# Casting two more weight groups by quarter lanes in a batched matmul, so that two loops cover 26 and 28 groups

## The chip, the cores and the metric

The kernel runs on one core of one Trainium2 chip. The metric is the device time of one execution in microseconds (us). A profile's span is some 1.8 us shorter than the time of the same execution (516.8 and 518.58 us for the kernel before), so spans are compared with spans and times with times. One run of the kernel before, at 660.4 us with a span of 658.6, counts as slow and is left out.

## The reference

```python
b1, b2, m, k, n = 8, 16, 256, 512, 384
x      = randn(b1, b2, m, k)  float32
weight = randn(b1, b2, k, n)  float32
out    = matmul(x, weight)    float32
```

There are 128 matrix products. The kernel takes four of them as one group, so there are 32 groups (`NG`), numbered 0 to 31.

## The kernel before

Each group loads 2048 KB of x and 3072 KB of weights, casts both to bf16, transposes x on TensorE, multiplies, and stores 1536 KB. The weights have two buffers (`WS = 2`), so group n can only be loaded when group n - 2 has been cast. All loads and stores are issued in program order on one queue, by SyncE.

The weights are cast in one of two forms. In the *long* form (`cast_w`, called by quarter lanes in the prediction) 16 casts of 32 partitions are shared: 11 on VectorE (`CV`) and 5 on ScalarE (`CA`), and the load is one transfer. In the *short* form (`cast_short`, by half lanes) 8 casts of 64 partitions run on VectorE alone, and the load is two transfers, so that the first four casts can start when the first half has landed. Before the change, groups 0 to 3, 30 and 31 are short.

```python
    def is_short(n):
        return isinstance(n, int) and (n < LAG or n >= NG - 2)      # LAG = 4

    def load_w(e, t, U, s):
        n = t * U + s
        if not isinstance(n, int) or n >= WS:
            e.wait_ge(w_vcast, n * CV + (1 - WS) * CV)              # group n-2 cast
            e.wait_ge(w_acast, n * CA + (1 - WS) * CA)
        d = SL // SH if is_short(n) else 1                          # two transfers or one
        ...

    def on_sync(e):
        ...
            for s in range(U):
                load_x(e, t, U, LAG + s)
                store(e, t, U, s)
                load_w(e, t, U, LAG + s)
        ...
        for n in range(NG - 1 - LAG, NG):                           # stores of 27 to 31
            store(e, 0, NG, n, T if n == NG - 1 else 1)             # the last in four pieces

    def on_vector(e):
        ...
        def step(t, U, s):
            n = t * U + s
            if is_short(n):
                cast_short(e, n)
            else:
                cast_w(e, t, U, s, range(XV))                       # 8 of the 11 casts
            if not isinstance(n, int) or n < NG - 1:
                next_x(t, U, s)                                     # x of group n+1
            if not is_short(n):
                cast_w(e, t, U, s, range(XV, CV), False)            # the other 3
        ...
        for n in range(LAG):
            step(0, NG, n)
        rounds = (NG - 3 - LAG) // U                                # 24 groups in the loop
        with e.Fori(0, rounds) as t:
            for s in range(U):
                step(t, U, LAG + s)
```

The store of a group waits for ScalarE's four copies out of PSUM. The store of group 31 goes out in four pieces of 384 KB, one after each copy.

Of the kernel before, what the change touches and what calls it, by code (L numbers as in the profile page):

```python
# [12 lines left out]
def kernel(  # L13
# [32 lines left out]
    NG = B // G  # L46

    XS, WS, OS = 2, 2, 4
    BS, TS, WBS = 1, 2, 2 * G
    PT, PO = 4, 2  # L50

    LAG = 4

    CA = 5
    CV = G * SL - CA
# [16 lines left out]
    def sems(name, n):  # L72
        return [tc.alloc_semaphore(f"{name}{s}") for s in range(n)]
# [23 lines left out]
    x_in, w_in, o_out = sems("x_in", XS), sems("w_in", WS), sems("o_out", OS)  # L97
# [6 lines left out]
    def load_x(e, t, U, s):  # L104
        n = t * U + s
        if not isinstance(n, int) or n >= XS:
            e.wait_ge(x_cast, n * T + (1 - XS) * T)
        e.dma_start(  # L108
            x_sb[s % XS][:],
            x_rows[bass.ds(n * (G * M), G * M)].rearrange("(p r) k -> p r k", r=R),  # L110
        ).then_inc(x_in[s % XS], 16)

    def is_short(n):
        return isinstance(n, int) and (n < LAG or n >= NG - 2)

    def load_w(e, t, U, s):
        n = t * U + s
        if not isinstance(n, int) or n >= WS:
            e.wait_ge(w_vcast, n * CV + (1 - WS) * CV)
            e.wait_ge(w_acast, n * CA + (1 - WS) * CA)  # L120
        d = SL // SH if is_short(n) else 1
        k = SL * KO // d
        for h in range(d):
            sem = h_in[s % WS * 2 + h] if is_short(n) else w_in[s % WS]
            e.dma_start(  # L125
                w_sb[s % WS][:, h * k : (h + 1) * k, :],
                w_rows[bass.ds(n * (G * K) + h * (G // d * K), G // d * K)].rearrange(
                    "(p k) n -> p k n", k=k
                ),
            ).then_inc(sem, 16)  # L130

    def store(e, t, U, s, pieces=1):
        n = t * U + s
        dram = o_rows[bass.ds(n * (G * M), G * M)].rearrange("(p r) n -> p r n", r=R)
        for q in range(pieces):
            rows = slice(q * R // pieces, (q + 1) * R // pieces)
            e.wait_ge(o_copied, n * T + ((q + 1) * T // pieces + BIAS))
            e.dma_start(out=dram[:, rows], in_=out_sb[s % OS][:, rows]).then_inc(
                o_out[s % OS], 16
            )  # L140

    def cast_x(e, t, U, s, q):
        n = t * U + s
        if q == 0:
            e.wait_ge(x_in[s % XS], (t * (U // XS) + s // XS) * 16 + 16)
        e.wait_ge(t_made, n * T + (q + 1 - T + BIAS))  # L146
        rows = slice(2 * q, 2 * q + 2)
        S = SH if is_short(n) else SL
        e.tensor_copy(  # L149
            out=x_bf[s % BS][:, rows].rearrange("p r (s q c) -> p r s q c", s=S, c=KO),  # L150
            in_=x_sb[s % XS][:, rows].rearrange("p r (q s c) -> p r s q c", s=S, c=KO),
        ).then_inc(x_cast, 1)

    def cast_w(e, t, U, s, parts, first=True):
        n = t * U + s
        if first:
            e.wait_ge(p_made, n * T + (BIAS - T))
            e.wait_ge(w_in[s % WS], (t * (U // WS) + (s - LAG) // WS) * 16 + 16)  # L158
        copy = e.tensor_copy if e is nc.vector else e.copy
        for c in parts:  # L160
            i, h = c // SL, c % SL
            copy(  # L162
                out=w_bf[(s * G + i) % WBS][h * C : (h + 1) * C],
                in_=w_sb[s % WS][i * C : (i + 1) * C, h * KO : (h + 1) * KO, :],
            ).then_inc(w_vcast if c < CV else w_acast, 1)

    def cast_short(e, n):
        e.wait_ge(p_made, n * T + (BIAS - T))
        p = P // SH
        for d in range(SL // SH):  # L170
            turns = n // WS if n < LAG else LAG // WS
            e.wait_ge(h_in[n % WS * 2 + d], turns * 16 + 16)  # L172
            for a in range(SH):
                for h in range(SH):
                    c = d * 4 + a * 2 + h
                    r = (d * SH + h) * KO

                    e.tensor_copy(  # L178
                        out=w_bf[(n * G + d * SH + a) % WBS][h * p : (h + 1) * p],
                        in_=w_sb[n % WS][a * p : (a + 1) * p, r : r + KO, :],  # L180
                    ).then_inc(w_vcast, 2 if c < CV - HV else 1)

    def evacuate(e, t, U, s):
        n = t * U + s
        e.wait_ge(p_made, n * T + (BIAS - T))
        for q in range(T):
            e.wait_ge(t_made, n * T + (q + 1 + BIAS))
            e.copy(  # L188
                out=x_t[s % TS][:, 2 * q : 2 * q + 2],
                in_=pt[(s * T + q) % PT][:].bitcast(bf16),  # L190
            ).then_inc(t_copied, 1)
# [36 lines left out]
    def copy_out(e, t, U, s, q):  # L228
        n = t * U + s
        if q == 0:  # L230
            e.wait_ge(o_out[s % OS], (t * (U // OS) + s // OS) * 16 + 16)
        e.wait_ge(p_made, n * T + (q + 1 + BIAS))
        e.copy(  # L233
            out=out_sb[s % OS][:, 2 * q : 2 * q + 2, :],
            in_=po[(s * T + q) % PO][:, :, :N],
        ).then_inc(o_copied, 1)
# [7 lines left out]
    def on_sync(e):  # L244
        U = OS
        for n in range(LAG):
            load_x(e, 0, NG, n)
            load_w(e, 0, NG, n)
        rounds = (NG - 2 - LAG) // U
# [4 lines that stand above are left out]
# [12 lines left out]
    def on_vector(e):  # L266
        U = 2

        def next_x(t, U, s):
            for q in range(T):  # L270
                cast_x(e, t, U, s + 1, q)
# [6 lines that stand above are left out]
                cast_w(e, t, U, s, range(XV))  # L278
            if not isinstance(n, int) or n < NG - 1:
                next_x(t, U, s)  # L280
            if not is_short(n):
                cast_w(e, t, U, s, range(XV, CV), False)

        next_x(0, NG, -1)
        for n in range(LAG):
            step(0, NG, n)
        rounds = (NG - 3 - LAG) // U
        with e.Fori(0, rounds) as t:  # L288
            for s in range(U):
                step(t, U, LAG + s)  # L290
        for n in range(LAG + rounds * U, NG):
            step(0, NG, n)

    def on_tensor(e):
# [14 lines left out]
    def on_scalar(e):  # L309
        U = OS  # L310
        e.sem_inc(t_copied, BIAS)
        e.sem_inc(o_copied, BIAS)
        for s in range(OS):
            e.sem_inc(o_out[s], 16)



        def step(t, U, s):
            short = is_short(t * U + s + 1)
            evacuate(e, t, U, s + 1)  # L320
            for q in range(T):
                copy_out(e, t, U, s, q)
                if q == 0 and short:
                    e.sem_inc(w_acast, CA)
                if q > 0 and not short:
                    last = CA if q == T - 1 else q
                    cast_w(e, t, U, s + 1, range(CV + q - 1, CV + last), q == 1)

        evacuate(e, 0, NG, 0)
        e.sem_inc(w_acast, CA)  # L330
        for n in range(LAG - 1):
            step(0, NG, n)
        rounds = (NG - 2 - LAG) // U
        with e.Fori(0, rounds) as t:
            for s in range(LAG - 1, LAG - 1 + U):
                step(t, U, s)
        for n in range(LAG - 1 + rounds * U, NG - 1):
            step(0, NG, n)
        for q in range(T):
            copy_out(e, 0, NG, NG - 1, q)  # L340

    on_gpsimd(nc.gpsimd)
    on_sync(nc.sync)
    on_vector(nc.vector)
    on_tensor(nc.tensor)
    on_scalar(nc.scalar)


# [28 lines left out]
```

## Time and profile before

In lines of a profile PE is TensorE and PEld its weight loads, DVE is VectorE, ACT is ScalarE, and SPq is SyncE issuing a transfer; L125 is a line of the kernel's file.

| | before |
|---|---|
| time, median of 3 runs | 518.49 us (518.26 to 518.54) |
| span of the profiled run | 516.8 us |
| TensorE, VectorE, ScalarE busy | 61%, 77%, 79% |
| data queue, share of 16 DMA engines | 99.0% (218.11 MB) |
| weight casts on VectorE: long, short | 286 of 951 ns, 48 of 955 ns |
| weight casts on ScalarE | 130 of 1468 ns |
| last copy out of PSUM ends | 506.57 us |
| last DMA increment lands | 515.3 us |

No engine computes after 506.57, and yet data moves for almost 9 us more. The trace also holds, for every transfer, 16 increments of its semaphore (1680 for 105 transfers). I read them as one for each of the 16 DMA engines, since in the tail 15 of the last piece's 16 are in at 512.28, the last comes at 515.31, and the DMA share between the two is 0.06, one engine of 16. The spread between the first and the last of them then tells how far the slowest engine lags.

### The profile page before, as it was taken

How to read it: one execution, taken by the hardware profiler on the slowest of the kernel's cores; microseconds unless marked ns; L12 is line 12 of the kernel's file. 1: busy time of each engine (PE TensorE's matmuls, PEld its weight loads, DVE VectorE, ACT ScalarE, POOL GpSimd, SP SyncE). 2: the span in 40 equal slices, each digit the busy share in tenths (PEclk: the TensorE clock that was granted, in tenths of full speed). 3: DMA queues.
4: the chain of work that ended last, by engine and by line, in shares of the span. 5: the costliest groups of instructions: out<-in, count | busy, mean ns of one | idle time of the engine just before them, and what ended most of it. 6: DMA issues, size and time to landing. Idle time of an engine off the chain costs nothing.

```text
span 516.8 us, 11572 instructions
## 1 busy us (share of the span) xinstructions
PE 315.2 (61%) x4608; PEld 225.4 (44%) x4608; DVE 397.7 (77%) x462; ACT 410.3 (79%) x387; POOL 0.7 (0%) x6
## 2 busy tenths in 40 slices
PE   2277838555676675765475766558656667565681
PEld 2255525444454443454353544435534445344550
DVE  2788757798777897777987778977779777797960
ACT  1365666998797989798979879978989897899561
POOL 0000000000000000000000000000000000000000
PEclk9687786878786778787778868776867786688887
DMA  8999999999999999999999999999999999999995
GB/s 335 426 428 425 435 429 423 431 430 434 429 424 431 432 439 434 424 426 433 434 434 431 422 432 433 435 429 428 425 438 429 440 428 420 433 433 429 424 428 219
DMA packets 15127, 218.19 MB, mean 422 GB/s; under 512 B 1680, under 2 KB 1680, under 8 KB 2192
## 3 DMA queue, kind: packets, MB, share of 16 engines
q1 hardware_dynamic: 15120, 218.11, 99.0%
q8 instruction: 3, 0.05, 0.0%
q14 instruction: 4, 0.03, 0.0%
HBM read 167.77 MB, written 50.33 MB: 422 GB/s over the span
## 4 chain that ended last, share of the span: by engine, by line
DMA 57%; DVE 29%; issue 9%; PE 1%; SPq 1%; DVEq 1%; ACT 0%
DMA w_sb<-in_weight_dram 57%; DVE w_bf L162 20%; DVE x_bf L149 5%; DVE w_bf L178 4%; PE po L219 1%; SPq L125 0%; DVEq L288 0%; SPq L108 0%; DVEq L158 0%; ACT out_sb L233 0%; SPq L120 0%; DVEq L146 0%; DVEq L172 0%; SPq L372 0%; SPq L60 0%
## 5 line engine op out<-in xcount | busy, mean ns | idle before, releaser
L162 DVE CAST w_bf<-w_sb 32x1536 bf16<-32x1536 f32 x286 | 271.9, 951 | 81.6 <-DMA w_sb<-in_weight_dram 73.5
L219 PE MATMUL po<-w_bf,x_t 128*32 128x384 bf16 x4096 | 200.6, 359 | 38.3 <-DVE w_bf L162 21.0
L201 PE MATMUL pt<-identity,x_bf 128*128 128x128 f32 x512 | 115.0, 415 | 152.2 <-DVE x_bf L149 152.2
L162 ACT CAST w_bf<-w_sb 32x1536 bf16<-32x1536 f32 x130 | 190.9, 1468 | 6.0 <-DMA w_sb<-in_weight_dram 2.8
L201 PEld LDWEIGHTS pt<-identity,x_bf 128*128 128x128 f32 x512 | 103.4, 224 | 164.1 <-issue 163.8
L219 PEld LDWEIGHTS po<-w_bf,x_t 128*32 128x32 bf16 x4096 | 122.0, 106 | 115.9 <-issue 40.7
L233 ACT COPY out_sb<-po 128x768 f32<-128x768 f32 x128 | 101.5, 803 | 57.3 <-PE po L219 56.6
L188 ACT COPY x_t<-pt 128x1024 bf16<-128x1024 bf16 x128 | 120.3, 1025 | 22.1 <-PE pt L201 21.5
L149 DVE CAST x_bf<-x_sb 128x1024 bf16<-128x1024 f32 x128 | 80.0, 688 | 12.4 <-DMA x_sb<-in_x_dram 11.5
L178 DVE CAST w_bf<-w_sb 64x1536 bf16<-64x1536 f32 x48 | 45.9, 955 | 8.3 <-DMA w_sb<-in_weight_dram 7.0
L188 ACT ACT_TABLE_LOAD x1 | 1.3, 1283 | 10.8 <-PE pt L201 10.8
masks.py:199 POOL TENSOR_SCALAR_AFFINE_SELECT identity<-identity 128x128 f32<-128x128 f32 x1 | 0.3, 294 | 0.2 <-POOL identity L239 0.2
L239 POOL MEMSET identity<- 128x128 f32 x1 | 0.2, 205 | 0.5 <-SPq L60 0.5
L361 POOL MEMSET const-bfloat16-1.0<- 128x1 bf16 x1 | 0.1, 102 | 0.0
L361 POOL MEMSET const-uint8-127<- 128x1 uint8 x1 | 0.1, 102 | 0.0
L361 POOL MEMSET const-float32-0.0<- 128x1 f32 x1 | 0.1, 99 | 0.2 <-issue 0.2
L361 POOL MEMSET const-float32-1.0<- 128x1 f32 x1 | 0.1, 99 | 0.0
## 6 DMA issues: line engine op xcount, KB each, us to landing
w_sb<-in_weight_dram SPq DMA_DIRECT2D x26, 3072.0 KB, 18.1
x_sb<-in_x_dram SPq DMA_DIRECT2D x32, 2048.0 KB, 22.3
out_dram<-out_sb SPq DMA_DIRECT2D x31, 1536.0 KB, 25.4
w_sb<-in_weight_dram SPq DMA_DIRECT2D x12, 1536.0 KB, 16.6
out_dram<-out_sb SPq DMA_DIRECT2D x4, 384.0 KB, 5.6
```

Source lines behind the costliest of these rows:

```text
L149: e.tensor_copy(out=x_bf[s % BS][:, rows].rearrange("p r (s q c) -> p r s q c", s=S, c=KO), in_=x_sb[s % XS][:, rows].rearrange("p r (q s ...
L162: copy(out=w_bf[(s * G + i) % WBS][h * C : (h + 1) * C], in_=w_sb[s % WS][i * C : (i + 1) * C, h * KO : (h + 1) * KO, :],).then_inc(w_vcas ...
L178: e.tensor_copy(out=w_bf[(n * G + d * SH + a) % WBS][h * p : (h + 1) * p], in_=w_sb[n % WS][a * p : (a + 1) * p, r : r + KO, :],).then_inc ...
L188: e.copy(out=x_t[s % TS][:, 2 * q : 2 * q + 2], in_=pt[(s * T + q) % PT][:].bitcast(bf16),).then_inc(t_copied, 1)
L201: ins = e.transpose(pt[(s * T + q) % PT][:, rr, h, :], words[:, 2 * q + rr, h :: KO // 2], identity[:],)
L219: ins = e.matmul(po[(s * T + q) % PO][mine, rr, :N], x_t[s % TS][:, 2 * q + rr, ko // 2, mine, ko % 2], w_bf[(s * G + i) % WBS][:, ko, :], ...
L233: e.copy(out=out_sb[s % OS][:, 2 * q : 2 * q + 2, :], in_=po[(s * T + q) % PO][:, :, :N],).then_inc(o_copied, 1)
L239: e.memset(identity[:], 0.0).then_inc(id_done, 1)
L361: nc = _bacc.Bacc("TRN2", target_bir_lowering=False, num_devices=1)
```

## The change

Its intent is less code: only groups 0, 1, 2 and 31 stay short, so group 3 can join both loops and group 30 ScalarE's, and the loops then cover 26 groups on VectorE and 28 on ScalarE (24 on each before).

```diff
+    HEAD = 3
...
     def is_short(n):
-        return isinstance(n, int) and (n < LAG or n >= NG - 2)
+        return isinstance(n, int) and not HEAD <= n < NG - 1
...
         if first:
-            e.wait_ge(w_in[s % WS], (t * (U // WS) + (s - LAG) // WS) * 16 + 16)
+            e.wait_ge(w_in[s % WS], (t * (U // WS) + (s - HEAD) // WS) * 16 + 16)
...
     def on_vector(e):
-        for n in range(LAG):
+        for n in range(HEAD):
             step(0, NG, n)
-        rounds = (NG - 3 - LAG) // U
+        rounds = (NG - 2 - HEAD) // U
...
     def on_scalar(e):
-        for n in range(LAG - 1):
+        for n in range(HEAD - 1):
             step(0, NG, n)
-        rounds = (NG - 2 - LAG) // U
+        rounds = (NG - 1 - HEAD) // U
```

(Cut: the loop ranges that follow from these, and the count of earlier short loads in `cast_short`, where `LAG` becomes `HEAD`.)

More of the change, by code (lines that the diff above doesn't have):

```diff
@@ L170, in cast_short @@
         for d in range(SL // SH):
-            turns = n // WS if n < LAG else LAG // WS
+            turns = n // WS if n < HEAD else HEAD // WS
             e.wait_ge(h_in[n % WS * 2 + d], turns * 16 + 16)
@@ L284, in on_vector @@
         next_x(0, NG, -1)
-        for n in range(LAG):
+        for n in range(HEAD):
             step(0, NG, n)
-        rounds = (NG - 3 - LAG) // U
+        rounds = (NG - 2 - HEAD) // U
         with e.Fori(0, rounds) as t:
-            for s in range(U):
-                step(t, U, LAG + s)
-        for n in range(LAG + rounds * U, NG):
+            for s in range(HEAD, HEAD + U):
+                step(t, U, s)
+        for n in range(HEAD + rounds * U, NG):
             step(0, NG, n)
@@ L330, in on_scalar @@
         e.sem_inc(w_acast, CA)
-        for n in range(LAG - 1):
+        for n in range(HEAD - 1):
             step(0, NG, n)
-        rounds = (NG - 2 - LAG) // U
+        rounds = (NG - 1 - HEAD) // U
         with e.Fori(0, rounds) as t:
-            for s in range(LAG - 1, LAG - 1 + U):
+            for s in range(HEAD - 1, HEAD - 1 + U):
                 step(t, U, s)
-        for n in range(LAG - 1 + rounds * U, NG - 1):
+        for n in range(HEAD - 1 + rounds * U, NG - 1):
             step(0, NG, n)
```

## The prediction

> **What bounds the kernel now.** I read the page first: the row of slices, the queues, then the chain that ended last.
>
> ```profile
> DMA  8999999999999999999999999999999999999995
> GB/s 335 426 428 425 435 429 423 431 430 434 429 424 431 432 439 434 424 426 433 434 434 431 422 432 433 435 429 428 425 438 429 440 428 420 433 433 429 424 428 219
> ...
> q1 hardware_dynamic: 15120, 218.11, 99.0%
> ...
> DMA 57%; DVE 29%; issue 9%; PE 1%; SPq 1%; DVEq 1%; ACT 0%
> ```
>
> The DMA engines are full in every slice but the first and the last, and the one data queue takes 99.0% of their time. VectorE (77%) and ScalarE (79%) have room. The chain mixes DMA 57% and VectorE 29% because weights are loaded into two buffers: a load is issued when the cast that empties its buffer ends, then lies some 18 us in the queue. That looks like a loop in which casts set the pace, but a load that waits behind other loads is not slowed by being issued later as long as the queue does not run dry. One group moves 2048 + 3072 + 1536 KB = 6.82 MB; at 429 GB/s that is 15.9 us, which is just the spacing of the weight loads in the timeline (449.25, 465.13, 481.03). So the bound is the number of bytes, and the change matters only if it (a) lets the queue run dry or (b) lengthens what comes after the last byte that the queue could have moved earlier. Group 3 lies at the head and group 30 at the tail, so I read the timeline there.
>
> Head:
>
> ```profile
> 58.84 0.33 SPq L125 DMA_DIRECT2D w_sb<-in_weight_dram  x1
> ...
> 70.09 7.83 DVE L162 CAST w_bf<-w_sb 32x1536 bf16<-32x1536 f32 x8 [8.43 <-DMA w_sb<-in_weight_dram]
> ...
> 83.67 0.33 SPq L125 DMA_DIRECT2D w_sb<-in_weight_dram  x1
> ```
>
> VectorE runs ahead of the queue there: it idles 8.43 us before group 4's weights land at 70.09. The load of group 5 goes out at 58.84, long before the queue needs it.
>
> Tail:
>
> ```profile
> 481.04 7.86 DVE L178 CAST w_bf<-w_sb 64x1536 bf16<-64x1536 f32 x8
> ...
> 492.24 7.86 DVE L178 CAST w_bf<-w_sb 64x1536 bf16<-64x1536 f32 x8 [0.80 <-DMA w_sb<-in_weight_dram]
> ...
> 500.34 5.39 PE L219 MATMUL po<-w_bf,x_t 128*32 128x384 bf16 x128 [1.46 <-DVE w_bf L178]
> ...
> 505.77 0.80 ACT L233 COPY out_sb<-po 128x768 f32<-128x768 f32 x1 [0.50 <-PE po L219]
> ```
>
> VectorE is busy through the last groups (from 488.93 to 491.43, between the two lines of casts, it casts group 31's x); the arithmetic ends at 506.57, yet the span ends at 516.8. The table of stretches says why:
>
> ```profile
> 509.00:510.00 1.00, 0.00 (x0) 0.00 (x0) 0.00 (x0) 0.00 (x0) 0.00 (x0) 1.00 0.92 372
> 510.00:511.00 1.00, 0.00 (x0) 0.00 (x0) 0.00 (x0) 0.00 (x0) 0.00 (x0) 1.00 0.45 181
> ...
> 512.00:513.00 1.00, 0.00 (x0) 0.00 (x0) 0.00 (x0) 0.00 (x0) 0.00 (x0) 0.50 0.06 25
> ...
> 514.00:515.00 1.00, 0.00 (x0) 0.00 (x0) 0.00 (x0) 0.00 (x0) 0.00 (x0) 0.50 0.05 22
> ```
>
> The DMA share (last but one column) is full to 510 and then 0.06, one of 16 engines, nearly to 515. The trace's packets end at 514.92 and the last semaphore increment is at 515.33. One engine is behind the others and has been busy without a break: its increments for the store of group 30 and the last store piece lie at 511.62 and 515.33, 3.71 us for four pieces, which is the pace of the bytes. So the end is set by the backlog of the slowest DMA engine, with the last copy hidden in front of it.
>
> [...] group 30's second weight half has its first increment at 479.4 and its last at 483.56. A wait for a whole load is therefore a wait for the slowest engine. [...] the trace has 951 ns for 32 lanes, 955 for 64 and 1468 on ScalarE, so [...] half as many lanes per cast is indeed no cheaper. [...] The page of before shows 7 packets and 0.08 MB on the instruction queues q8 and q14, of 218 MB, so shorter code cannot give much.
>
> **The change part by part.** Groups 3 and 30 leave the half-lane form. For each, 8 casts of 955 ns (7.6 us) on VectorE become 11 of 951 (10.5 us) there and 5 of 1468 (7.3 us) on ScalarE; two loads of 1536 KB become one of 3072 KB, so the first cast waits for all of it. In all VectorE gets +5.6 us and ScalarE +14.7 us of busy time.
>
> *Transfers.* Per engine and group, 16 packets of 12288 bytes (460 ns in the trace) become 8 of 24576 (912 ns): 16 x 460 - 8 x 912 = 64 ns, and one semaphore write of 9 ns less. Two groups: -0.15 us, which counts in full, as this is the bound. (A quarter-lane cast covers 32 partitions, a half-lane one 64.)
>
> *Head, group 3.* Its halves land complete at 50.6 and 54.3 (increments). VectorE starts at 54.3 instead of 50.7; 8 casts x 0.98 = 7.8 gives 62.1, group 4's x casts (landed at 59.2) 2.5 gives 64.7, three more casts end at 67.6. ScalarE, with five casts between its copies, ends near 65. The multiply of group 3 starts near 67.7, not 63.35, and group 5's weight load is issued near 67.6, not 58.84: 8.8 us later. Does the queue run dry? The fastest engine finishes what precedes that load (store of group 1) at 76.7 and a load needs about 1.05 us from issue to first packet (0.96 to 2.01 at the start): it must be out by 75.6. 8 us remain. Group 4's weights land at 70.1 as before, VectorE, idle since 67.6, starts its casts then, and from there the schedule is the old one. Worth 0.
>
> *Tail, group 30.* VectorE is ready at 481.04 but the whole load lands at 483.56: +2.55. Eleven casts for eight: +2.95. The 0.80 wait for group 31's first half (landed at 492.14) vanishes: -0.80. Sum +4.7: group 31's casts end near 504.8, its multiply runs 505.0 to 510.4, the last copy ends near 511.3 instead of 506.57. ScalarE's casts end near 494 and the transposes of group 31 near 496, ahead of that. The last piece, issued at 511.3 and met by an idle queue, would need 1.05 to its first packet, 8 packets x 121 ns = 0.97, and 0.41 to the increment (514.92 to 515.33): 513.7. The slowest engine is not there before 515.2. So 4.7 us of longer work fits into the slack, with 1.5 us to spare; the other 15 engines get a hole of 1 to 2 us before the store of group 30 that nobody waits for.
>
> Sum: -0.15 us, and perhaps -0.1 for fewer instruction fetches, which are guesswork: 518.49 - 0.2 = 518.3.
>
> **Rivals.** *The tail is exposed.* If the slowest engine's lag is an accident of this profile (it lost about 1.4 us to one slow packet near 423), the last copy becomes the end. For: all engines but that one are done by about 512.3. Then before ends about 2.6 us earlier too, while the runs (518.26 to 518.54) and the profiled one (518.58) are alike, so the lag seems usual. A smaller lag in the new kernel alone would end it at 513.7 + 1.45 (515.33 to 516.8) = 515.2 of span, 1.6 faster: 516.9. A tail longer than I think (a lower granted clock on the last multiplies, as the 0.5 near 512 warns; a later landing) gives +1 to +2: 520. *VectorE becomes the bound:* 5.6 us more in series would be 524; against it, it idles 8.43 us at the head and 2.4 to 2.9 us per group before weights. *The code itself:* loop entries and exits move by a group, [...]. If the fetch near 422 caused the slow packet near 423 and goes away, -1.4 us.
>
> **Range and chances.** The gains end at about 1.6 us, the losses that I can name at about 1.5 beyond 518.5: 517.0 to 520.0. Two per cent is 10.4 us, which no rival reaches: 0.01 faster, 0.98 same, 0.01 slower.
>
> **What would show it.** In the page, 308 quarter-lane casts on VectorE (286 before), 140 on ScalarE (130) and 32 half-lane ones (48); the load of group 5 near 67.6 with a full DMA share between 60 and 90; the casts of group 4 still at 70.1; group 30's first cast near 483.6; the last copy ending near 511.3; a DMA share that stays near one engine until about 515. The prediction is wrong if the share dips at the head, or if the last store piece starts on an idle queue and the span follows the last copy.

(What no trace or run of this case shows is cut and marked. None of it was a term of the sum, which came to -0.2 us. That a load issued later is not slowed while the queue has work is measured below: group 5's load went out 8.9 us later and group 4's casts started at 70.11 instead of 70.09.)

## The result, and the profile after

The changed kernel takes 518.79 us (median of 4 runs, 518.75 to 518.83) beside 518.38 us (518.12 to 518.54) of the kernel before: ratio 1.0008, interval 0.9991 to 1.0026: *same*, inside the predicted range and 0.5 us above the predicted number. Timed again later beside other kernels it took 518.63 us and the kernel before 518.45 us (ratio 1.0004, 0.9991 to 1.0018).

First the page of the changed kernel: the DMA rows of the slices, the data queue, and the shares of the chain that ended last (the profile's path of waits, followed back from the last instruction).

```profile
DMA  8999999999999999999999999999999999999986
GB/s 337 424 431 427 429 433 417 438 428 439 423 427 434 431 436 434 427 424 432 430 432 432 427 430 433 438 430 427 422 435 430 434 435 418 434 431 442 416 381 249
...
q1 hardware_dynamic: 14832, 218.11, 98.9%
...
DMA 57%; DVE 32%; issue 7%; PE 1%; DVEq 1%; SPq 0%; ACT 0%
```

The slices are full from the second to the last but one, as before; the rate of the last two slices went from 428 and 219 GB/s to 381 and 249: a little work has moved later. Next the groups of casts on the same page (busy us, mean ns of one, then idle time before them).

```profile
L163 DVE CAST w_bf<-w_sb 32x1536 bf16<-32x1536 f32 x308 | 292.8, 951 | 83.9 <-DMA w_sb<-in_weight_dram 75.1
...
L163 ACT CAST w_bf<-w_sb 32x1536 bf16<-32x1536 f32 x140 | 205.5, 1468 | 3.5
...
L179 DVE CAST w_bf<-w_sb 64x1536 bf16<-64x1536 f32 x32 | 30.6, 955 | 5.9 <-DMA w_sb<-in_weight_dram 5.0
```

The counts are those that the change asks for: 308 long casts on VectorE and 140 on ScalarE, 32 short ones, each at its old duration. VectorE is 5.7 us busier in all (397.7 to 403.4) and ScalarE 14.3 us (410.3 to 424.6). None of that is to be found in the time.

The head, in the timeline of the changed kernel (start, us, engine, line, operation, in brackets the idle time before it):

```profile
67.76 0.33 SPq L126 DMA_DIRECT2D w_sb<-in_weight_dram  x1
...
70.11 7.83 DVE L163 CAST w_bf<-w_sb 32x1536 bf16<-32x1536 f32 x8 [2.61 <-DMA w_sb<-in_weight_dram]
...
83.68 0.33 SPq L126 DMA_DIRECT2D w_sb<-in_weight_dram  x1
```

Group 5's weight load goes out at 67.76 instead of 58.84, and still group 4's casts start at 70.11 (70.09 before) and group 6's load goes out at 83.68 (83.67 before). In the stretches from 50 to 100 the DMA share is 0.97 to 1.04. The 8.9 us were spare.

The tail, in the same view:

```profile
483.66 7.83 DVE L163 CAST w_bf<-w_sb 32x1536 bf16<-32x1536 f32 x8 [2.61 <-DMA w_sb<-in_weight_dram]
...
496.99 7.86 DVE L179 CAST w_bf<-w_sb 64x1536 bf16<-64x1536 f32 x8
...
505.09 5.38 PE L220 MATMUL po<-w_bf,x_t 128*32 128x384 bf16 x128 [2.52 <-DVE w_bf L179]
...
510.52 0.80 ACT L234 COPY out_sb<-po 128x768 f32<-128x768 f32 x1 [0.50 <-PE po L220]
```

Group 30's casts start 2.6 us later, group 31's 4.75 us later, its multiply likewise, and the last copy ends at 511.32 instead of 506.57. The stretches of the changed kernel (from:to, length, then busy us and count on TensorE, its weight loads, VectorE, ScalarE and GpSimd, the granted clock, the DMA share, GB/s):

```profile
502.00:504.00 2.00, 0.57 (x16) 0.13 (x8) 1.94 (x3) 0.91 (x2) 0.00 (x0) 1.00 0.35 147
...
511.00:512.00 1.00, 0.00 (x0) 0.00 (x0) 0.00 (x0) 0.32 (x1) 0.00 (x0) 1.00 0.85 341
...
513.00:514.00 1.00, 0.00 (x0) 0.00 (x0) 0.00 (x0) 0.00 (x0) 0.00 (x0) 0.77 0.21 83
514.00:515.00 1.00, 0.00 (x0) 0.00 (x0) 0.00 (x0) 0.00 (x0) 0.00 (x0) 0.50 0.07 28
```

and one of the kernel before, for the same time:

```profile
502.00:504.00 2.00, 2.00 (x56) 1.48 (x52) 0.00 (x0) 1.53 (x2) 0.00 (x0) 1.00 1.03 436
```

Two things are to be seen. From 502 to 504 the DMA share falls from 1.03 to 0.35: most DMA engines have done all that was issued and wait for the store of group 30, which waits for copies that are now later. And from 514 to 515 the share is 0.07, one engine of 16, as before. The increments show why the hole costs next to nothing:

| last increment of the slowest DMA engine, us | before | after |
|---|---|---|
| group 31, second weight half | 495.78 | 495.79 |
| store of 27 | 499.91 | 499.75 |
| store of 28 | 503.95 | 503.83 |
| store of 29 | 507.90 | 507.76 |
| store of 30 | 511.60 | 511.82 |
| last piece of 31 | 515.31 | 515.56 |
| last piece of 31 on the first engine | 509.95 | 513.49 |

(The prediction read the same increments 0.02 to 0.03 us later. The trace does not name an increment's engine; the first engine's is the one that follows its earlier pieces at their pace.) The first engine to finish finishes 3.5 us later, the slowest 0.25 us later. The slowest is level at 495.8 in both. It loses its 0.25 us in one place, the store of group 30, which takes it 4.06 us instead of 3.70, less 0.1 to 0.2 us that it had gained in the store of 27. So the lag of one DMA engine swallows a tail that is 4.75 us longer, and a rest of a quarter of a microsecond comes out of one store.

### The profile page after: what moved, and what is told of

Its sections match the earlier page's. It is cut to its first block, busy times and chain, and to the rows that moved or that the text cites. A ratio compares the mean times of both kernels' runs of the same rounds, so it can differ in the third digit from the quotient of the medians.

```text
span 517.0 us, 11608 instructions
## 1 busy us (share of the span) xinstructions
PE 321.4 (62%) x4608; PEld 227.7 (44%) x4608; DVE 403.4 (78%) x468; ACT 424.6 (82%) x397; POOL 0.7 (0%) x6
## 4 chain that ended last, share of the span: by engine, by line
DMA 57%; DVE 32%; issue 7%; PE 1%; DVEq 1%; SPq 0%; ACT 0%
DMA w_sb<-in_weight_dram 57%; DVE w_bf L163 24%; DVE x_bf L150 5%; DVE w_bf L179 3%; PE po L220 1%; DVEq L289 0%; SPq L126 0%; DVEq L159 0%; ACT out_sb L234 0%; DVEq L147 0%; SPq L121 0%; SPq L109 0%; DVEq L173 0%; SPq L373 0%; SPq L61 0%
## 5 line engine op out<-in xcount | busy, mean ns | idle before, releaser
L163 DVE CAST w_bf<-w_sb 32x1536 bf16<-32x1536 f32 x308 | 292.8, 951 | 83.9 <-DMA w_sb<-in_weight_dram 75.1
L220 PE MATMUL po<-w_bf,x_t 128*32 128x384 bf16 x4096 | 205.7, 366 | 42.2 <-DVE w_bf L163 22.0
L163 ACT CAST w_bf<-w_sb 32x1536 bf16<-32x1536 f32 x140 | 205.5, 1468 | 3.5
L220 PEld LDWEIGHTS po<-w_bf,x_t 128*32 128x32 bf16 x4096 | 124.1, 107 | 123.4 <-issue 43.8
L179 DVE CAST w_bf<-w_sb 64x1536 bf16<-64x1536 f32 x32 | 30.6, 955 | 5.9 <-DMA w_sb<-in_weight_dram 5.0
```

The source lines that it names most:

```text
L163: copy(out=w_bf[(s * G + i) % WBS][h * C : (h + 1) * C], in_=w_sb[s % WS][i * C : (i + 1) * C, h * KO : (h + 1) * KO, :],).then_inc(w_vcas ...
L179: e.tensor_copy(out=w_bf[(n * G + d * SH + a) % WBS][h * p : (h + 1) * p], in_=w_sb[n % WS][a * p : (a + 1) * p, r : r + KO, :],).then_inc ...
L220: ins = e.matmul(po[(s * T + q) % PO][mine, rr, :N], x_t[s % TS][:, 2 * q + rr, ko // 2, mine, ko % 2], w_bf[(s * G + i) % WBS][:, ko, :], ...
```

## The experiments

The theories, as the runs' expectations name them. **A**: the slowest DMA engine has work to the end, this sets the time of both kernels, and the longer tail only shows where it outlasts that engine; the small loss comes from the tail (first version: because the other 15 engines, which pass through the hole, do their last stores later and slow the slowest one). **B**: the small loss comes from the head, where group 3's casts and the following loads are later. **C**: the last copy sets the end in both kernels. A fourth, **D**, came out of the first traces and is told where it was tested.

### Each half of the change alone

Only group 3 long (diff against the changed kernel):

```diff
-        return isinstance(n, int) and not HEAD <= n < NG - 1
+        return isinstance(n, int) and not HEAD <= n < NG - 2
...
-            turns = n // WS if n < HEAD else HEAD // WS
+            turns = n // WS if n < HEAD else (HEAD + 1 - n % WS) // WS
...
-        rounds = (NG - 2 - HEAD) // U      # VectorE
+        rounds = (NG - 3 - HEAD) // U
...
-        rounds = (NG - 1 - HEAD) // U      # ScalarE
+        rounds = (NG - 2 - HEAD) // U
```

> Only group 3 is made long; groups 30 and 31 stay in half lanes. Theory A (the slowest DMA engine's backlog sets the end; the small loss comes from the tail): time as before, 518.2 to 518.5, ratio 0.9995 to 1.0002; group 5's weight load out near 67.7, casts of group 4 at 70.1, last copy ending near 506.5. Theory B (the small loss comes from the later loads at the head): 518.7 to 518.9, ratio about 1.0008.

It took 518.5 us beside 518.42 us of the kernel before: ratio 0.9999 (0.9985 to 1.0012). Its timeline has group 5's load as late as the changed kernel, and the last copy where the kernel before has it:

```profile
67.83 0.33 SPq L126 DMA_DIRECT2D w_sb<-in_weight_dram  x1
```

```profile
505.81 0.80 ACT L234 COPY out_sb<-po 128x768 f32<-128x768 f32 x1 [0.50 <-PE po L220]
```

The interval alone would still leave room for B's 0.4 us; the trace does not: its last increment lies at 515.34, beside 515.31 of the kernel before. A load that goes out 9 us later costs nothing here: B falls.

Only group 30 long:

```diff
-    HEAD = 3
+    HEAD = 4
```

> Only group 30 is made long; group 3 stays in half lanes. Theory A: 518.7 to 518.9, ratio about 1.0008, a hole in the DMA share at 502.6 to 504.6 and the last copy ending near 511.3. Theory B: 518.2 to 518.5, though the last copy is just as late.

518.69 us, ratio 1.0006 (0.9992 to 1.0019). The last copy ends at 511.17, and the hole is there (stretches, the last two columns are DMA share and GB/s):

```profile
502.00:504.00 2.00, 1.10 (x28) 0.54 (x20) 1.94 (x3) 1.44 (x2) 0.00 (x0) 1.00 0.38 158
```

The medians put the small loss in the tail, as A has it, though the interval of this run alone includes none at all.

### Filling the hole

The changed kernel with the store of group 30 in four pieces:

```diff
-            store(e, 0, NG, n, T if n == NG - 1 else 1)
+            store(e, 0, NG, n, T if n >= NG - 2 else 1)
...
-            e.wait_ge(o_out[s], 16 + 16 * (NG // OS + (T - 1 if s == (NG - 1) % OS else 0)))
+            e.wait_ge(o_out[s], 16 + 16 * (NG // OS + (T - 1 if s >= (NG - 2) % OS else 0)))
```

> The changed kernel with the store of group 30 in four pieces, so that the 15 quicker engines need not wait for its last copy. Theory A, second part (their later work slows the slowest engine, whose share of group 30's store took 4.06 us instead of 3.70): hole at 502.6 to 504.6 filled, the slowest engine's store of group 30 nearer 3.8 us, time 518.4 to 518.7, 0.1 to 0.3 below the changed kernel. If the loss is something else, or the last copy sets the end: 518.8 as the changed kernel, hole filled or not.

518.84 us, ratio 1.0008 (0.9994 to 1.0022): no gain. The hole was filled, and another opened behind it:

```profile
502.00:504.00 2.00, 1.10 (x28) 0.54 (x20) 1.94 (x3) 1.45 (x2) 0.00 (x0) 1.00 0.94 383
...
506.00:508.00 2.00, 2.00 (x56) 1.48 (x52) 0.00 (x0) 0.99 (x2) 0.00 (x0) 1.00 0.34 134
```

The share from 502 to 504 is 0.94 instead of 0.35. The slowest engine's increments lie at 507.70 after the store of 29 and at 511.84 after that of 30, 4.14 us apart: no faster than with the hole. The second part of A, as I had put it, falls: when the other DMA engines do their last stores makes no difference.

### How much slack each kernel has

To see what sets the end I took bytes away: the store of group 28 is left out, so that block of the output is never written and the result is wrong. The same edit was made in both kernels:

```diff
         for n in range(NG - 1 - LAG, NG):
+            if n == NG - 4:
+                continue
             store(e, 0, NG, n, T if n == NG - 1 else 1)
...
-            e.wait_ge(o_out[s], 16 + 16 * (NG // OS + (T - 1 if s == (NG - 1) % OS else 0)))
+            e.wait_ge(o_out[s], 16 + 16 * (NG // OS + (T - 1 if s == (NG - 1) % OS else 0) - (s == 0)))
```

> The kernel before without the store of group 28 (a wrong result on purpose: that block of the output is never written). Theory A: the slowest engine loses its 3.95 us of that store and still sets the end, since the last copy (506.6) plus 2.2 to 2.4 us lies at 509: time 518.4 - 3.9 = 514.3 to 514.8. Theory C (last copy sets the end): 518.4, unchanged.

> The changed kernel without the store of group 28 (wrong on purpose in that block). Theory A: the slowest engine would end near 511.7, but the last copy ends at 511.3 and its piece lands on every engine near 513.5, so only the slack of about 2 us is gained: 516.6 to 517.2, some 2.2 slower than the kernel before with the same cut. If the chain of casts is irrelevant even then: 514.7. Theory C: 518.8, unchanged.

The kernel before fell to 514.56 us beside 518.3 (ratio 0.9928, 0.9914 to 0.9942): 3.7 us, all that a store costs the slowest engine when nothing slows it (3.70 for the store of group 30 above). The changed kernel fell only to 517.36 us (ratio 0.998 against the kernel before, 0.9966 to 0.9994), some 1.3 us below its own time and 0.2 us above the range that I had given. The stretches, first of the kernel before without that store, then of the changed one:

```profile
510.00:512.00 2.00, 0.00 (x0) 0.00 (x0) 0.00 (x0) 0.00 (x0) 0.00 (x0) 0.50 0.03 11
```

```profile
502.00:504.00 2.00, 2.00 (x52) 1.09 (x44) 1.94 (x3) 1.09 (x2) 0.00 (x0) 1.00 0.02 6
...
512.00:514.00 2.00, 0.00 (x0) 0.00 (x0) 0.00 (x0) 0.00 (x0) 0.00 (x0) 1.00 0.72 286
```

In the first, one engine of 16 is still the last to finish (0.03 is one engine for half of the stretch): bytes set the end even with one store fewer. In the second the DMA engines stand still from 502 to 504 (0.02) and then all end together near 514 (0.72 from 512 to 514). From 506 to 512 their share is 0.95 to 1.01: once group 30's last copy is done (504.90) they move the last two stores without a break, so here that copy and the bytes behind it set the end, and not the last copy (510.98), as I had expected. C falls for both kernels as they are. Of the bytes taken away the changed kernel could use some 1.3 us, the kernel before all 3.7.

### Using the slack up

The changed kernel with group 31 long too, which makes the tail longer still:

```diff
-        return isinstance(n, int) and not HEAD <= n < NG - 1
+        return isinstance(n, int) and not HEAD <= n < NG
```

> The changed kernel with group 31 long too. ScalarE then casts five parts of group 31 between its copies, so I expect group 31's multiply to start near 509.5 and the last copy to end near 515.7, 4.4 us later than in the changed kernel. Theory A: of that only what exceeds the slack shows: the last piece needs 2.2 to 2.4 us after its issue, so it lands near 518 and the span ends near 519.5, time 521.0 to 521.6, about 2.5 above the changed kernel. Theory C (the last copy sets the end in both kernels already): 523.2, all of the 4.4. If the end were set by the bytes alone: 518.8.

525.06 us (523.66 to 525.2), ratio 1.0129 (1.0113 to 1.0144), slower than I had expected. The profiled run is the one of 523.66:

```profile
505.36 4.45 ACT L163 CAST w_bf<-w_sb 32x1536 bf16<-32x1536 f32 x3
...
510.15 7.09 PE L220 MATMUL po<-w_bf,x_t 128*32 128x384 bf16 x128 [7.56 <-ACT w_bf L163]
...
517.29 0.80 ACT L234 COPY out_sb<-po 128x768 f32<-128x768 f32 x1 [0.50 <-PE po L220]
```

ScalarE ends its casts of group 31 at 509.81, so the multiply starts at 510.15, 0.65 us later than I had worked out, and it took 7.09 us instead of 5.38 (the granted clock, 1.00 under the changed kernel's last multiply, was 0.50 here from 508 to 512 and 0.59 in the next two microseconds), so the last copy ends at 518.09, 6.8 us later than in the changed kernel. The span grew by 4.9 us (517.0 to 521.9): 1.9 us of the 6.8 were hidden, and all 16 DMA engines finish together, at 520.24 to 520.42. The multiply's length, which I had taken from a run at full clock, was the larger mistake; that the excess over the slack shows is what A says. The 1.9 us are also what the table above gives for the changed kernel, from the quicker engines' last increments (513.49 to 513.65) to the slowest one's (515.56). The other three timed runs are 1.4 us longer than the profiled one, and I have no profile of them.

### Using up the slack at the head

The changed kernel with only group 0 short at the head:

```diff
-    HEAD = 3
+    HEAD = 1
```

> The changed kernel with only group 0 of the head in half lanes (groups 1 and 2 long too). By the same working as for group 3, group 3's weight load goes out near 43.1, when the queue has nothing left after 43.5, so there is at most 1 us of dry queue, and group 4's near 56.4 with 2 us to spare. Theory A (a late load costs only the dry time): 518.8 to 519.8, with a dip of the DMA share near 43. If lateness of the loads itself costs (VectorE as a bound at the head): 4 to 6 us more, 523 or above.

520.01 us (519.5 to 520.12), ratio 1.0028 (1.0014 to 1.0042), some 1.2 us above the changed kernel and 0.2 us above what I had allowed. The loads went out at 42.92 and 56.49, within 0.2 us of the working. The queue of the DMA issues, and stretches behind the first and around the second:

```profile
56.49 0.35 SPq L126 DMA_DIRECT2D w_sb<-in_weight_dram  x1
```

```profile
45.00:46.00 1.00, 1.00 (x32) 0.73 (x28) 0.97 (x2) 0.56 (x2) 0.00 (x0) 1.00 0.87 369
...
56.00:58.00 2.00, 1.55 (x40) 1.11 (x44) 1.94 (x3) 2.00 (x3) 0.00 (x0) 1.00 0.69 197
```

Only a small part of the loss is where I looked for it: behind the first late load the rate dips from 44 to 47 (369 GB/s at 45), and by the bytes moved this kernel falls back by a quarter of a microsecond there. The rest, some 0.9 us, is lost from 55 to 58, where the rate falls to 197 GB/s while the share reads 0.69: packets of group 4's x took up to 2.1 us there instead of 0.61. Why they did is open; apart from them the queue held only one store and, from 56.49 on, this load. Still, VectorE worked without a pause from 29.6 to 69.6 in this kernel and the time rose by 1.2 us, not by the 4 to 6 us that VectorE as a bound would give.

### A faster way to share out the bytes

If one DMA engine is last by about 3 us (515.31 for 512.28 in the kernel before), giving it fewer bytes should beat both kernels. I assumed, without a run that showed it, that a split of a store by partitions would take bytes away from one engine. So I split the store of group 28 in the kernel before:

```diff
-            e.dma_start(out=dram[:, rows], in_=out_sb[s % OS][:, rows]).then_inc(
-                o_out[s % OS], 16
-            )
+            for lanes in ((slice(0, 120), slice(120, P)) if isinstance(n, int) and n == NG - 4 else (slice(0, P),)):
+                e.dma_start(out=dram[lanes, rows], in_=out_sb[s % OS][lanes, rows]).then_inc(
+                    o_out[s % OS], 16
+                )
```

(and the last wait on that slot counts 16 more.)

("That one" is the engine that I supposed would be relieved.)

> The kernel before with the store of group 28 issued as 120 partitions and 8 partitions, [...]. If the slowest engine is that one: its end moves 3.9 us earlier and the next slowest sets the end near 512.7 instead of 515.3, time 515.8 to 516.4, faster than both kernels with a right result. If the slowest is another engine: 518.3 to 519.0.

523.2 us, ratio 1.0093 (1.0079 to 1.0108): 4.9 us slower, and a miss. The stretch:

```profile
496.00:500.00 4.00, 1.95 (x48) 1.18 (x40) 3.87 (x5) 1.60 (x2) 0.00 (x0) 1.00 1.02 365
```

The rate falls to 365 GB/s at a full share. Between 496 and 508, 38 packets of 12288 bytes took over 700 ns, 17 of them 900 to 952, where the kernel before has none (the median is 460 in both), and the last increment came at 519.98. The trace shows 25 increments for the two transfers, two of them at the issues (482.93 and 483.30), where a whole store has 16. How the bytes were shared out among the engines is not shown; what is shown is that packets became slow. Which engine is the slowest stays open, and so does a way to relieve it. No version with a right result that I ran beats both kernels.

### What slows the slowest DMA engine

With the hole ruled out, I looked at the store packets in all traces. Nearly all of them take 460 ns, but in the tail there are some of 505 to 550 ns, about one in each half microsecond, as a single engine would produce them. Their times match TensorE's multiplies:

| | multiplies at the end | store packets over 505 ns |
|---|---|---|
| before | to 498.9; 500.34 to 505.7 | 495.8 to 498.4; 500.8 to 505.0 |
| after | 497.2 to 502.6; 505.1 to 510.5 | 497.6 to 502.4; 505.7 to 509.8 |

(A single one of 666 ns, at 499.2 in the kernel before, stands right behind an instruction fetch at 498.9, on another engine: the slowest engine's packets run on across it without a gap.) The same holds in the middle of the run, where I had not looked for it: from 72 to 478 us of the kernel before, 13 of the 1319 store packets under a multiply take 505 to 560 ns, and none of the 1817 that lie outside all work of TensorE. There they stand in a row up to a multiply's end (137.08 to 138.63, for one that ends at 138.9). **D**: TensorE's multiplies slow that engine's stores. In the changed kernel the two last multiplies both lie over the five stores; in the kernel before 3 us of the earlier one lie in front of them. To test it I gave the kernel before useless work at its end, on TensorE in one kernel, on ScalarE in the other:

```diff
             multiply(e, t, U, 1)
+        for q in range(6):
+            for rr in range(2):
+                for ko in range(KO):
+                    for i in range(G):
+                        mine = slice(i * C, (i + 1) * C)
+                        e.matmul(
+                            pt[q % PT][mine].rearrange("p a b c -> p (a b c)")[:, :N],
+                            x_t[1][:, 2 * (q % T) + rr, ko // 2, mine, ko % 2],
+                            w_bf[(G + i) % WBS][:, ko, :], start=(ko == 0), stop=(ko == KO - 1))
```

> The kernel before with 192 useless matmuls on TensorE after its last multiply (into banks that nobody reads, so the result stays right), about 8 us, from 505.8 to near 513.9. In the traces so far the slowest DMA engine's store packets of 12288 bytes take 505 to 550 ns instead of 460 just while TensorE multiplies. If that is a cause and not a coincidence (theory D), the store of group 30 on that engine takes about 4.1 us instead of 3.70 and the rest a little longer: time 518.8 to 519.4, 0.4 to 1.0 above the kernel before. If TensorE has nothing to do with it: 518.3 to 518.5.

```diff
             copy_out(e, 0, NG, NG - 1, q)
+        for q in range(8):
+            spare = x_t[0] if q < T else x_bf[0]
+            e.copy(out=spare[:, 2 * (q % T) : 2 * (q % T) + 2], in_=pt[q % PT][:].bitcast(bf16))
```

> The control for it: the kernel before with eight useless copies on ScalarE after its last copy (about 8 us, 506.6 to near 514.9, into buffers that nobody reads any more), TensorE idle. Theory D: 518.3 to 518.5, as before, and store packets of 460 ns after 505.8. If any engine's work at the end slows the slowest DMA engine, or if a later end of the arithmetic is what counts: 518.7 to 519.4.

The extra work, in the timeline of each:

```profile
505.36 7.99 PE L313 MATMUL pt<-w_bf,x_t 128*32 128x384 bf16 x192
```

```profile
506.35 3.77 ACT L343 COPY x_t<-pt 128x1024 bf16<-128x1024 bf16 x4
509.96 3.82 ACT L343 COPY x_bf<-pt 128x1024 bf16<-128x1024 bf16 x4
```

With TensorE busy to 513.35 the kernel took 519.4 us beside 518.45: ratio 1.0021 (1.0007 to 1.0034). The slow packets now go on without a gap to 510.9, the store of group 30 took the slowest engine 4.19 us, and the last piece came at 515.90 (515.31 in the kernel before). With ScalarE busy to 513.78 it took 518.45 us, ratio 1.0004 (0.999 to 1.0017); the last slow packet is at 505.2 and the store of group 30 took 3.70 us. (The extra matmuls also brought one more instruction fetch, of 0.88 us at 509.6; it is not on the slowest engine, whose packets of 509.36, 509.90 and 510.42 follow each other without a gap.) D holds: it is TensorE's multiplies, not work as such and not a later end of the arithmetic. The kernel before without the store of group 28 agrees: the store of group 30, moved forward under the last multiply, took the slowest engine 3.99 us there instead of 3.70. What in the multiplies does it, and why on that engine only, is not shown: the control has 8 instructions where TensorE has 192 matmuls and as many weight loads, so their mere number, or what is fetched or recorded for them, is not ruled out.

How the lag came about can be read from the increments of the kernel before. From its first to its last increment a transfer took 2.1 us near 70 us, 3.2 near 419, 3.9 near 425, behind an instruction fetch, 4.1 at 495.8 and 5.3 at 507.9: the last step is the stores under the two last multiplies.

In the two last kernels' company the changed kernel was timed again, unaltered:

> The changed kernel unaltered, timed again beside the kernel before and the two above on one chip, as the first interval (0.9991 to 1.0026) does not tell 0.4 us from nothing. Theory A with D: 518.6 to 518.9, ratio 1.0005 to 1.0010. If the 0.4 us was noise: ratio 0.9997 to 1.0003.

518.63 us, ratio 1.0004 (0.9991 to 1.0018). Four timings with group 30 long (the changed kernel twice, group 30 alone, the store in pieces) gave 1.0008, 1.0004, 1.0006 and 1.0008, the one with group 3 alone 0.9999. The sign is always the same, but no single interval leaves out 1, so the loss is 0.2 to 0.4 us by the medians and not proven by the times. The traces agree with it: the last increment is 0.25 us later in the first profile of the changed kernel and 0.34 in the second.

## Why the prediction was right

*The bound.* Bytes on the slowest DMA engine set the end, as predicted: the kernel before without one store gained all of its 3.7 us.

*Transfers, -0.15 us.* It cannot be seen: at 495.8 the slowest engine stood level in both traces. The term is smaller than what the profiles differ by.

*Head, 0.* Right to within 0.2 us on VectorE, the loads and the multiply (load at 67.76 for 67.6, multiply at 67.73 for 67.7, group 4's casts at 70.11 for 70.1); ScalarE's casts, for which it had 65, ended at 64.25. And the kernel with this half of the change alone gave 0.9999.

*Tail, +4.7 us on the engines.* Right: 4.75 us, with its parts (casts from 483.66 for 483.6, the multiply from 505.09 for 505.0, the last copy ending at 511.32 for 511.3).

*"So 4.7 us of longer work fits into the slack, with 1.5 us to spare".* Right: the changed kernel's own increments leave 1.9 us, and 1.9 us of a still longer tail were hidden; with one store less the changed kernel gained about 1.3 us.

*"the other 15 engines get a hole of 1 to 2 us before the store of group 30 that nobody waits for".* The hole is there and indeed nobody waits for it. But I took it that a longer tail within the slack is worth exactly 0. That term was mis-sized: +0.25 us in the trace. The slowest engine is not independent of the arithmetic, since its store packets take some 525 ns rather than 460 while TensorE multiplies, and the change moved about 2.3 us more of multiply over the stores (from 495.8 on, 3.1 + 5.4 us before and 5.4 + 5.4 after). At 65 ns for each 525 that is 0.28 us, an estimate from those packets.

*Fetches, -0.1, called guesswork.* No gain is seen. The page shows 3 instead of 4 packets on the queue q14, as the one at 498.9 is gone, but that one had not touched the slowest engine. (Its store of 27 took 4.13 us before and 3.96 after because seven of its eight packets took 502 to 545 ns under a multiply before, and only three 512 to 545 ns after.) The fetch near 422 was not removed, it moved to 435.3, and the packet behind it again took 1.02 us instead of 0.61. The prediction's "it lost about 1.4 us to one slow packet near 423" was too much: the packet's excess is 0.41 us and the fetch itself 0.31, and the spread of the increments grew there by 0.7 us (3.16 to 3.86; after the change 3.39 to 4.06).

*Rival, the exposed tail.* Its "before ends about 2.6 us earlier too" is 3.0 us by the increments (512.28 to 515.31).

The sum was -0.2 us and the medians give +0.2 to +0.4; the one term that is missing has been shown by experiment, though only its sign and size and not what in the multiplies makes it; and the rivals (VectorE as the bound, the exposed tail) did not happen.

## What to carry to other kernels

In a kernel that is bound by transfers, work out for each stage when the queue would run dry and when the last transfer could start at the earliest; here 5.7 us of VectorE and 14.3 us of ScalarE stayed within those two times, and the medians put their cost at 0.2 to 0.4 us. Look at the slowest of the DMA engines, not at their mean, since here it decided when a load counted as landed (group 30's in the changed kernel has its first increment at 479.25 and its last at 483.57, and its casts started at 483.66) and when the kernel ended (515.56, with the other engines done by 513.65). And test slack by taking bytes away: the kernel before, which gained all 3.7 us of them, is bound by bytes; the changed one, which gained 1.3 us, has a chain right behind.
